# The first product of a feed-forward by seven products of quarters for five of eleven pairs of tiles, with the order of all engines written down

## The chip, the cores and the metric

One core of one Trainium2 chip runs the whole program in one launch. The metric is the device time of that launch in microseconds (us), taken as the median of several executions; a profiled execution, which has a time of its own, gives the trace. The engines are PE (matrix products), DVE (vector), ACT (scalar functions and copies), POOL (a second vector engine) and SP (which issues the DMAs).

## The reference

The program is a decoder of two layers, each a half feed-forward, a mixer and another half feed-forward, on 512 positions of 1024 features:

```python
def swiglu_ffn(x, norm_g, w_in, w_out):
    gate, up = jnp.split(rms_norm(x, norm_g) @ w_in, 2, axis=-1)
    return (jax.nn.silu(gate) * up) @ w_out
...
    for layer in range(DEPTH):
        x = x + 0.5 * swiglu_ffn(x, ffn_pre_norm[layer], ffn_pre_w_in[layer], ffn_pre_w_out[layer])
        ...            # mixer: RWKV-7 (layer 0) or dilated attention (layer 1), and attention to a memory
        x = x + y
        x = x + 0.5 * swiglu_ffn(x, ffn_post_norm[layer], ffn_post_w_in[layer], ffn_post_w_out[layer])
        if layer == N_A_LAYERS - 1:
            k_blocks, v_blocks = shared_kv_blocks(x, kv_norm, kv_w, kv_k_norm)
```

The inner width of a feed-forward is 2816, so `w_in` is 1024 x 5632 and `w_out` 2816 x 1024. All is fp32. The four feed-forwards are called 00, 01, 10 and 11 (layer, then before or after its mixer).

## The kernel before

The state x lies transposed: eight tiles of 128 features x 512 positions (part j of x is features 128 j to 128 j + 127). Weights are cut into tiles of 128 columns; a tile of the first product has eight blocks of 128x128, one for each part of x, and is loaded in two halves of four blocks (`raw`, 128x512, 256 KB).

**Split products.** PE multiplies in a rounded fp32 form, so every operand is split in a high and a low part: ACT copies it to the rounded form (`whi`, `uh`, `hh`), and DVE or POOL subtracts that from the original (`wlo`, `ul`, `hl`). Each product is then three matmuls: high by high, high of the weights by low of x, low of the weights by high of x. `weight` (line 383) loads and splits one half tile, the low part by turns on DVE and POOL; `dense` (line 401) issues the three matmuls for each block.

**A feed-forward** (`ffn`, line 444). The first product has 22 tiles of gate columns and 22 of up columns. For each m of 22 the gate tile and the up tile go through 8 blocks x 3 matmuls of 128x512 each into two banks. The square sum of x, kept by `Operand.squares`, is turned by `Operand.rstd` into the reciprocal root `r` of every position, spread on 128 partitions: one fp32 matmul of 512 columns with ones, a root on ACT, a reciprocal of 128x512 on DVE. Gating is DVE (gate times `r`, `gs`), ACT (Silu), DVE (times up, `hm`), and the hidden tile is split. The second product has eight output tiles of 22 blocks x 3 matmuls; `add_state` (line 427) scales the result, adds the old part of x, which is read again from memory (`xin`), makes the high and low parts of the next normed operand, and stores the part (`xd`).

**Beside the products.** Keys and values of the memory (256 positions) come from 96 matmuls with 256 columns, after the second product in feed-forward 00 and near the end of the first product in 01 (`memory_operand`, `memory_kv`). Feed-forward 01 also computes the position bias (`bias_rows`), and 10 reads its input again as the operand of the shared keys (`reload`: `kvh`, `kvl`). Mixer B starts from that operand and its own. At the end of each mixer, `lead` splits the first four half tiles of the next feed-forward.

**What sets the order.** Each engine runs its own list of instructions in order and waits by semaphores. The lists come from the tile framework's scheduler, which places the recorded instructions by their data and the buffers that come free; inside a mixer, `weave` with `Meter`'s costs sets the order in which strands are recorded. Weights have 6 buffers of `raw` and 4 each of `whi` and `wlo`; the feed-forward has 8 banks (`fps`).

## Time and profile before

| what | us |
|---|---|
| median of three runs (lowest, highest) | 2134.4 (2134.18, 2135.02) |
| time of the profiled execution | 2133.36 |
| its span, first to last instruction | 2131.6 |
| PE busy in the span | 2065.4 |
| feed-forward 00, from 6.2 | 379.8 |
| mixer A, from 386.0 | 419.4 |
| feed-forwards 01 and 10, from 805.4 | 740.3 |
| mixer B, from 1545.7 | 218.3 |
| feed-forward 11, from 1764.0 | 362.9 |

A row of a timeline gives the start, the length, engine, line, operation and tiles, and in brackets the idle time before it and who ended that. A row of a group gives the count (x), the busy time in all and the mean in ns, then idle time before its instructions by who ended it. The record of a matmul is longer than its share of the time, since matmuls overlap: the distance between starts is what one costs in a row of many. "L278" is the line of the helper through which every instruction of this kernel is issued (in the changed kernel the same helper is at line 309), so groups are told apart by their tiles.

### The profile page before, as it was taken

Reading aid. Unit: us, or ns where it says so; the run is one execution under the profiler, and the core shown is the slowest. Engines: PE = TensorE matmul, PEld = TensorE weight load, DVE = VectorE, ACT = ScalarE, POOL = GpSimd, SP = SyncE. Lnnn points to the kernel's source line nnn. Section 1 sums busy time; section 2 is a strip of 40 time slices with the busy share of each in tenths; the row PEclk is TensorE's granted clock in tenths of the full one; section 3 lists DMA queues with packets and bytes.
Section 4 is the critical chain, followed back from the end, with each engine's and each line's share of the span. In section 5 each row is a group of like instructions: output and inputs, shape, how many; then the busy total and the mean of one; then the engine's idle time right before and its main releaser. Section 6 shows DMA issues by size and latency. Waiting matters only on the chain.

```text
span 2131.6 us, 32197 instructions
## 1 busy us (share of the span) xinstructions
PE 2065.4 (97%) x12734; PEld 1651.9 (77%) x12734; DVE 983.3 (46%) x1354; ACT 817.6 (38%) x1408; POOL 583.1 (27%) x502
## 2 busy tenths in 40 slices
PE   8999999979989899999999999999999999999999
PEld 6888888857666577778888888888877667888887
DVE  6333343575767747333434533324376675333322
ACT  6333333423333545333433433333345654333321
POOL 2222222643332133222222222222242224222221
PEclk9999999999999999999999999999999999999999
DMA  5322344311100045253344423234441144222342
GB/s 194 97 97 96 92 136 126 117 46 34 34 27 24 24 152 188 93 183 99 109 127 126 158 95 98 95 94 135 125 136 50 38 161 156 96 97 96 94 136 82
DMA packets 130632, 221.90 MB, mean 104 GB/s; under 512 B 14232, under 2 KB 31824, under 8 KB 130480
## 3 DMA queue, kind: packets, MB, share of 16 engines
q1 hardware_dynamic: 130480, 219.83, 32.8%
q8 instruction: 100, 1.64, 0.3%
q14 instruction: 52, 0.43, 0.1%
HBM read 202.89 MB, written 21.61 MB: 105 GB/s over the span
## 4 chain that ended last, share of the span: by engine, by line
PE 62%; DVE 2%; ACT 1%; issue 1%; DMA 0%; POOL 0%; SPq 0%; POOLq 0%; ACTq 0%; DVEq 0%
PE fps L278 50%; PE mm L278 6%; PE sc L278 4%; PE py L278 1%; DMA xin<-xd 0%; DVE prob L278 0%; DVE x L278 0%; DVE tmp L278 0%; DVE ul L278 0%; ACT krv L278 0%; DVE wlo L278 0%; DVE dmx L278 0%; POOL wlo L278 0%; DVE mpr L278 0%; ACT tmp L278 0%
## 5 line engine op out<-in xcount | busy, mean ns | idle before, releaser
L278 POOL TENSOR_TENSOR wlo<-raw,whi 128x512 fp32r<-128x512 f32 (+3 forms) x404 | 496.3, 1230 | 1439.7 <-ACT whi L278 1395.2
L278 ACT ACTIVATE whi<-raw 128x512 fp32r<-128x512 f32 (+3 forms) x684 | 416.1, 610 | 955.1 <-PE fps L278 778.7
L278 PE MATMUL fps<-uh,whi 128*128 128x512 f32 x1408 | 551.9, 392 | 7.6 <-ACT whi L278 7.6
L278 PE MATMUL fps<-uh,wlo 128*128 128x512 f32 x1408 | 550.0, 391 | 4.0 <-DVE wlo L278 2.4
L278 PE MATMUL fps<-ul,whi 128*128 128x512 f32 x1408 | 549.2, 390 | 0.0
L278 DVE TENSOR_TENSOR wlo<-raw,whi 128x512 fp32r<-128x512 f32 x280 | 201.2, 719 | 347.0 <-ACT whi L278 337.3
L278 PEld LDWEIGHTS fps<-uh,whi 128*128 128x128 f32 x1408 | 264.9, 188 | 68.3 <-ACT whi L278 11.1
L278 PEld LDWEIGHTS fps<-uh,wlo 128*128 128x128 f32 x1408 | 264.9, 188 | 62.0 <-DVE wlo L278 4.1
L278 PEld LDWEIGHTS fps<-ul,whi 128*128 128x128 f32 x1408 | 265.0, 188 | 56.0 <-issue 0.7
L278 PE MATMUL fps<-hh,whi 128*128 128x512 f32 x704 | 273.9, 389 | 0.0
L278 PE MATMUL fps<-hl,whi 128*128 128x512 f32 x704 | 273.9, 389 | 0.0
L278 PE MATMUL fps<-hh,wlo 128*128 128x512 f32 x704 | 273.9, 389 | 0.0
L278 DVE TENSOR_TENSOR gs<-fps,rstd 128x512 f32<-128x512 f32 x88 | 60.5, 690 | 322.9 <-PE fps L278 322.9
L278 PEld LDWEIGHTS fps<-hh,whi 128*128 128x128 f32 x704 | 132.1, 188 | 27.5
L278 PEld LDWEIGHTS fps<-hh,wlo 128*128 128x128 f32 x704 | 132.1, 188 | 27.4
L278 PEld LDWEIGHTS fps<-hl,whi 128*128 128x128 f32 x704 | 132.1, 188 | 27.4
L278 PE MATMUL mm<-uh,whi 128*128 128x512 f32 x280 | 120.6, 431 | 1.3 <-DVE x L278 0.9
L278 DVE TENSOR_TENSOR hm<-fps,gs 128x512 f32<-128x512 f32 x88 | 60.6, 691 | 121.5 <-PE fps L278 115.8
L278 PE MATMUL mm<-ul,whi 128*128 128x512 f32 x280 | 114.7, 410 | 1.1 <-DVE ul L278 1.1
L278 PE MATMUL mm<-uh,wlo 128*128 128x512 f32 x280 | 113.3, 405 | 0.0
L278 DVE RECIPROCAL tmp<-tmp 128x128 f32<-128x128 f32 x112 | 97.8, 918 | 29.1 <-ACT tmp L278 29.0
L278 DVE TENSOR_TENSOR hl<-hm,hh 128x512 fp32r<-128x512 f32 x88 | 76.9, 877 | 50.7 <-ACT hh L278 50.7
(256 smaller groups left out, 2115.5 us busy)
## 6 DMA issues: line engine op xcount, KB each, us to landing
raw<-w SPq DMA_DIRECT2D x512, 256.0 KB, 2.7
raw<-wa_in SPq DMA_DIRECT2D x44, 256.0 KB, 3.0
xd<-x SPq DMA_DIRECT2D x40, 256.0 KB, 3.8
tmp<-xd SPq DMA_DIRECT2D x32, 256.0 KB, 3.7
xin<-xd SPq DMA_DIRECT2D x32, 256.0 KB, 4.2
raw<-w_kv SPq DMA_DIRECT2D x24, 256.0 KB, 2.8
raw<-w SPq DMA_DIRECT2D x32, 128.0 KB, 2.3
raw<-wmem SPq DMA_DIRECT2D x16, 256.0 KB, 2.6
```

Source lines behind the costliest of these rows:

```text
L278: r = f(*args, **kw)
```

## The change

**The products.** In the first product of each feed-forward, five of the eleven pairs of hidden tiles (p = 1, 3, 5, 7, 9; a pair has two gate and two up tiles) are computed by seven products of quarters in place of eight. The quarters of the weights of one m are "11" and "12" (gate, even and odd parts of x) and "21" and "22" (up); x is quartered into even and odd parts, first and second half of the positions. Sums of weight quarters (S1 = 21 + 22, S2 = S1 - 11, S3 = 11 - 21, S4 = 12 - S2) are made on POOL, from further loads (`sraw`). Each product is two jobs, one for each m of the pair, of four blocks x three matmuls of 128x256. Sums of the results are formed by ACT copies and DVE additions. The other six pairs (class `Whole`) keep 128x512 matmuls; their x of an even part holds the first half and the difference of the second half to the first, and `copy` and `finish` undo that difference.

**The operands.** An even part of x is split in two halves (`Operand.add` with `turns`), and three turned operands t2, t3, t4 are built early in the feed-forward (`turns`: x is loaded again, then per two parts an ACT scaling, three DVE instructions, two ACT copies and two DVE subtractions).

**The order.** `ffn` records under a manual schedule: every engine's list is the order in which the code is written, job by job. A job is one half tile and its twelve matmuls. Weights are loaded up to eight jobs ahead and split three jobs ahead (`ahead, loads = 3, 8`). All low parts of a feed-forward's weights are on DVE. Jobs 0 to 7 are both first tiles (even parts, then odd), jobs 8 to 11 a third tile, and the first pair begins at job 12; between the products of a pair one job of a whole tile is put.

**The root.** `column` uses four fp32 matmuls of one column, a root and a reciprocal of 128x4, and `spread` four fp32 matmuls of 128x128 that put it on 128 partitions, and a copy on ACT.

**What moves.** The memory's products and keys go between output tiles of the second product (00 and 01); the bias rows to the second product of 01 in nine parts of 256 columns, and their copies to that of 10; the loading of the shared keys' operand from feed-forward 10 to the start of mixer B. Feed-forward 10's first half tiles are split at the end of 01 (`follow`).

The diff, cut to its core:

```diff
@@ class Operand
+        if self.turns and j % 2 == 0:
+            d = net.xp.tile([P, TH], F32, tag="turn", bufs=1, name=net.nm("turn"))
+            net.split_into(h[:, :TH], l[:, :TH], x[:, :TH], gain)
+            nc.vector.tensor_tensor(d, x[:, TH:], x[:, :TH], op=ALU.subtract)
+            net.split_into(h[:, TH:], l[:, TH:], d, gain)
+        else:
+            net.split_into(h, l, x, gain)
...
-        nc.tensor.matmul(ps[:, :n], net.ones, self.acc, start=True, stop=True)
+        for b in range(n // P):
+            nc.tensor.matmul(ps[:, b:b + 1], self.acc[:, b * P:(b + 1) * P], net.ones[:, :1], start=True, stop=True,
...
+    def spread(self, c, ps):
+        for b in range(n // P):
+            nc.tensor.matmul(ps[:, b * P:(b + 1) * P], c[:, b:b + 1].broadcast_to([P, P]), net.ident, start=True,
...
@@ class Net
+    def both(self, raw, eng=None):
+        self.nc.scalar.activation(hi, raw, AF.Copy)
+        (eng or self.nc.vector).tensor_tensor(lo, raw, hi.bitcast(F32), op=ALU.subtract)
...
+            act.activation(a, a, AF.Copy, scale=self.v(gain, 2 * i))
+            yield
+            vec.scalar_tensor_tensor(b[:, 1], b[:, 1], g, a[:, 1], op0=ALU.mult, op1=ALU.subtract)
+            vec.tensor_tensor(a[:, 0], b[:, 1], a[:, 0], op=ALU.add)
+            vec.scalar_tensor_tensor(b[:, 0], b[:, 0], g, a[:, 0], op0=ALU.mult, op1=ALU.subtract)
...
+            form = {1: ("11", b11), 2: ("12", b21), 3: ("S4", b22), 5: ("S1", t1)}
...
+                def sum(q, i, n):
+                    a, b, op = {"S1": ("21", "22", ALU.add), "S2": ("S1", "11", sub), "S3": ("11", "21", sub),
+                                "S4": ("12", "S2", sub)}[n]
+                    t = self.take(hp, [P, WB, P], F32, "S", 6)
+                    gp.tensor_tensor(t, q.S[i, a], q.S[i, b], op=op)
...
+                    elif n == 6:
+                        q.s2 = tile_g()
+                        vec.tensor_tensor(q.s2, q.Y(), q.s1, op=ALU.add)
+                    elif n == 7:
+                        vec.tensor_tensor(q.s3, q.Y(), q.s1, op=ALU.add)
+                        vec.tensor_tensor(q.s3, q.Z(), q.s3, op=ALU.add)
...
+            seven = [p for p in range(1, NF // 2) if p % 2 == 1 and p < NF // 2 - 1]
+            order = (1, 5, 2, 6, 7, 4, 3)
...
+                for n in order:
+                    starts[p, n] = len(jobs)
+                    jobs += q.jobs(n)
+                    if others and (n != 1 or p == seven[0]):
+                        jobs.append(others.pop(0))
...
+            ahead, loads = 3, 8
...
+                if c + ahead < len(jobs) and c + ahead >= 8:
+                    both(jobs[c + ahead])
+                if j.then:
+                    j.then()
...
+                elif 5 < c < 16:
+                    for i in range(KD // 2):
+                        if 0 <= c - 6 - 2 * i < 4:
+                            next(steps[i], None)
@@ mixer_b
+            run(self.reload(ukv, src))
```

The lists of three engines in the first product of feed-forward 11 show where things now stand. PE, before, at the end of one tile's chain and the start of the next (`fps` is a bank, `uh` and `ul` the parts of x):

```order
L278 MATMUL fps_15951<-ul_15736,whi_16008 128x512
L278 MATMUL fps_15951<-uh_15735,wlo_16009 128x512
L278 MATMUL fps_15951<-uh_15741,whi_16008 128x512
L278 MATMUL fps_15951<-ul_15742,whi_16008 128x512
L278 MATMUL fps_15951<-uh_15741,wlo_16009 128x512
L278 MATMUL fps_16033<-uh_15617,whi_16037 128x512
```

PE, now, within the first pair, at the end of one job and the start of the next, whose weights are a sum:

```order
L309 MATMUL fps_19032<-ul_18174,whi_19002 128x256
L309 MATMUL fps_19032<-uh_18173,wlo_19003 128x256
L309 MATMUL fps_19076<-uh_18043,whi_19025 128x256
L309 MATMUL fps_19076<-ul_18044,whi_19025 128x256
L309 MATMUL fps_19076<-uh_18043,wlo_19026 128x256
```

The matmuls of a pair have half the columns and one job has twelve of them. DVE, before, just behind the reciprocal of the root (`gs` and `hm` gate, `hl` is a hidden low part):

```order
L278 RECIPROCAL rstd_15929<-rstd_15929 128x512
L278 TENSOR_TENSOR wlo_16038<-raw_16035,whi_16037 128x512
L278 TENSOR_TENSOR gs_15932<-fps_15803,rstd_15929 128x512
L278 TENSOR_TENSOR gs_15941<-fps_15805,rstd_15929 128x512
L278 TENSOR_TENSOR hm_15935<-fps_15804,gs_15932 128x512
L278 TENSOR_TENSOR hm_15944<-fps_15806,gs_15941 128x512
```

DVE, now, a stretch of the 32 instructions between the first turning step and the low part of job 15 (`h` of 256 columns is a turning step or gating, `tl` a turned low part):

```order
L309 TENSOR_TENSOR wlo_18479<-raw_18346,whi_18478 128x512
L309 TENSOR_TENSOR wlo_18509<-raw_18348,whi_18508 128x512
L309 TENSOR_TENSOR tl_18485<-h_18257,th_18484 128x512
L309 TENSOR_TENSOR tl_18487<-h_18257,th_18486 128x256
L309 SCALAR_TENSOR_TENSOR h_18256<-h_18256,vec 128x256
L309 TENSOR_TENSOR h_18256<-h_18256 128x256
L309 SCALAR_TENSOR_TENSOR h_18256<-h_18256,vec 128x256
L309 TENSOR_TENSOR wlo_18538<-raw_18363,whi_18537 128x512
L309 TENSOR_TENSOR g_18482<-fps_18457,g_18482 128x256
L309 TENSOR_TENSOR h_18249<-fps_18457,rstd_18451 128x256
L309 TENSOR_TENSOR h_18249<-g_18482,rstd_18451 128x256
L309 TENSOR_TENSOR wlo_18568<-raw_18398,whi_18567 128x512
```

Between two low parts there now stand the steps of the turned operands and the gating in halves. POOL, before, at the same place, has every second low part of the weights:

```order
L278 TENSOR_TENSOR wlo_16009<-raw_16006,whi_16008 128x512
L278 TENSOR_TENSOR wlo_16056<-raw_16053,whi_16055 128x512
L278 TENSOR_TENSOR wlo_16092<-raw_16089,whi_16091 128x512
L278 TENSOR_TENSOR wlo_16139<-raw_16136,whi_16138 128x512
L278 TENSOR_TENSOR wlo_16175<-raw_16172,whi_16174 128x512
```

POOL, now (`S` is a sum; the row of `h` is a hidden low part):

```order
L309 TENSOR_TENSOR S_18532<-sraw_18412,sraw_18414 128x512
L309 TENSOR_TENSOR S_18563<-sraw_18434,sraw_18436 128x512
L309 TENSOR_TENSOR h_18535<-h_18247,hh_18534 128x512
L309 TENSOR_TENSOR S_18617<-S_18532,sraw_18470 128x512
L309 TENSOR_TENSOR S_18643<-sraw_18470,sraw_18412 128x512
L309 TENSOR_TENSOR S_18670<-S_18563,sraw_18506 128x512
L309 TENSOR_TENSOR S_18690<-sraw_18506,sraw_18434 128x512
```

POOL's low parts have gone to DVE, and sums and hidden low parts stand in their place.

More of the change, by code (lines that the diff above doesn't have):

```diff
@@ new lines, in ffn @@
+            last_turn = starts[seven[-1], 3]
+            jobs += others
+            n1 = len(jobs)
+            there = {m: max(c for c, j in enumerate(jobs) if j.m == m) + 4 for m in range(NF)}
+            at = 0
+            for m in range(NF):
+                early = m < NF - 2 * slots
+                at = max(at + (10 if early else m % 2), there[m], 0 if early else last_turn)
+                mark(at, lambda e=gp if early or m % 2 else vec: split_hidden(e))
+            before, products, after = second(tmp, extra) if second else ((), [], ())
@@ L504, in memory_kv @@
[L504 to L519 removed]
+        have, ps = {}, {}
@@ L1217, in trunk, with rest @@
+                    return tuple(t[:, j % 2] for t in tiles[j - j % 2])
+                before, products, after = net.memory(layer, tmp, bank, place, out)
+                def rest():
+                    yield from after
+                    if more:
+                        yield from more(tmp, lambda t: bank())
+                return before, products, rest()
+            return pool, out, parts
         nxt = Operand(net, "g0m")
-        pool, kv, before, after = memory(0)
+        pool, kv, steps = memory(0)
```

515 lines of the change are left out of this document (391 added, 124 removed).

## The prediction

> **What bounds the kernel now.** I read the page's first part, then busy time by stage, then the waits of PE.
>
> ```profile
> span 2131.6 us, 32197 instructions
> PE 2065.4 (97%) x12734; PEld 1651.9 (77%) x12734; DVE 983.3 (46%) x1354; ACT 817.6 (38%) x1408; POOL 583.1 (27%) x502
> ...
> 0.00:6.20 6.20, 0.00 (x0) 0.00 (x0) 0.75 (x1) 3.25 (x5) 0.34 (x6) 1.00 0.61 182
> 6.20:386.00 379.80, 377.42 (x1693) 312.11 (x1693) 149.04 (x204) 148.40 (x246) 95.04 (x76) 1.00 0.39 121
> 386.00:805.40 419.40, 379.99 (x5061) 279.73 (x5060) 270.81 (x396) 160.26 (x303) 151.20 (x148) 0.98 0.18 58
> 805.40:1545.70 740.30, 739.70 (x3289) 608.18 (x3288) 286.76 (x375) 270.28 (x443) 180.19 (x146) 1.00 0.39 121
> 1545.70:1764.00 218.30, 207.61 (x1112) 154.61 (x1111) 153.07 (x222) 118.49 (x226) 65.12 (x57) 1.00 0.32 100
> 1764.00:2126.90 362.90, 360.49 (x1587) 297.29 (x1585) 121.45 (x156) 116.87 (x188) 91.24 (x73) 1.00 0.34 107
> ...
> PE fps L278 <- ACT whi L278: 7.6, 2, 6.2
> PE fps L278 <- DVE wlo L278: 2.4, 2, 1.6
> ```
>
> After 6.2 us of loads the five stretches are the first feed-forward, mixer A, the second and third feed-forwards, mixer B and the last feed-forward; the columns are length, then busy time of PE, PEld, DVE, ACT and POOL, granted clock, DMA share, GB/s. The feed-forwards fill 1483.0 us, and PE is busy in 1477.6 of them: only PE's own work can be cut there, and any new wait of PE is added in full. The clock is 1.00, so a shorter wait of PE buys nothing back. The two wait rows say how little PE waits for split weights today. The profiled execution took 2133.36 us for a span of 2131.6; it lies 1.0 under the median of 2134.4, and the sum below is made against it.
>
> **The products, the one gain.** For four 128-column tiles the kernel now issues 4 x 8 x 3 = 96 matmuls with 512 columns of x; a pair by seven products issues 7 x 2 x 4 x 3 = 168 with 256. So all hangs on the pitch of the two widths. Both stand in the first feed-forward (PE's timeline; the second width in the memory keys):
>
> ```profile
> 329.69 0.39 PE L278 MATMUL fps<-hh,whi 128*128 128x512 f32 x1
> ...
> 339.89 0.39 PE L278 MATMUL fps<-hh,whi 128*128 128x512 f32 x1
> ...
> 373.21 0.28 PE L278 MATMUL fps<-mh,whi 128*128 128x256 f32 x1
> ...
> 379.44 0.28 PE L278 MATMUL fps<-ml,whi 128*128 128x256 f32 x1
> ...
> L278 PEld LDWEIGHTS fps<-mh,wlo 128*128 128x128 f32 x64 | 12.3, 192 | 0.0
> ```
>
> Of 512 columns there are 46 rows from the first to the last, (339.89 - 329.69) / 45 = 0.2267 us apart; of 256 there are 53, (379.44 - 373.21) / 52 = 0.1198 us. The weight load of 192 ns does not set the narrow pitch: loads overlap. A pair costs 168 x 0.1198 = 20.13 us and not 96 x 0.2267 = 21.76, 1.64 less. Five pairs in four feed-forwards: **-32.7 us**. The other six pairs keep their 96 matmuls.
>
> [...]
>
> **The root of the mean square.** One fp32 matmul of 512 columns becomes four that make a column (128x1) and, after a reciprocal, four that spread it (128x128).
>
> ```profile
> 827.87 1.02 PE L278 MATMUL fps<-sq,cst 128*128 128x512 f32 x2
> 828.33 0.80 PE L278 MATMUL fps<-uh,whi 128*128 128x512 f32 x1
> 828.97 0.40 PE L278 MATMUL fps<-ul,whi 128*128 128x512 f32 x1
> ...
> 1054.03 0.60 PE L278 MATMUL fps<-cst,mt 128*128 128x128 f32 x4
> 1054.39 0.48 PE L278 MATMUL fps<-uh,whi 128*128 128x512 f32 x1
> ```
>
> The old one takes 828.97 - 827.87, less the one matmul between at 0.2267, so 0.87 us. The spread has the same 512 fp32 columns and is put at the same 0.87. The column is new: an fp32 matmul leaves two records (the x2 above), so eight, for which the nearest row is the four of 128x128 at (1054.39 - 1054.03) / 4 = 0.09 a record: 0.72 us. Six full ones and two of half width: 6 x 0.72 + 2 x 0.36 = **+5.0** (ends +2, if a 128x1 record costs a third of that; +12, if each of its 28 matmuls costs half an old one, 0.435). In the feed-forwards two weight jobs stand between column and spread, 5.4 us of cover (a job is one tile of weights, four blocks by three matmuls: 12 x 0.2267 = 2.72 us at 512 columns, 1.44 at 256). In mixer A the order puts only three matmuls (0.68 us) between column and spread, while ACT's root, DVE's reciprocal and three hand-overs lie between them; I add **+0.7** (0 to 2). The old reciprocal of 512 columns on DVE goes, off PE's path.
>
> **The early stretch of each feed-forward.** This is where I expect the loss. All low parts of its weights move to DVE, POOL gets the sums S1 to S4 of weight quarters, and in jobs 6 to 15 DVE also builds the turned operands and gates the first two tiles at once. Prices of the pieces (busy, mean ns of one):
>
> ```profile
> L278 DVE TENSOR_TENSOR wlo<-raw,whi 128x512 fp32r<-128x512 f32 x280 | 201.2, 719 | 347.0 <-ACT whi L278 337.3 <-PE fps L278 9.3
> L278 DVE TENSOR_TENSOR gs<-fps,rstd 128x512 f32<-128x512 f32 x88 | 60.5, 690 | 322.9 <-PE fps L278 322.9
> L278 DVE TENSOR_TENSOR mt<-fps,rstd 128x256 f32<-128x256 f32 x8 | 3.4, 422 | 7.8 <-PE fps L278 7.8
> L278 DVE SCALAR_TENSOR_TENSOR ml<-mt,vec,mh 128x256 fp32r<-128x256 f32 x16 | 7.9, 501 | 6.2 <-ACT mh L278 6.1
> L278 POOL TENSOR_TENSOR wlo<-raw,whi 128x512 fp32r<-128x512 f32 x340 | 447.6, 1317 | 1223.1 <-ACT whi L278 1182.3 <-PE mm L278 16.1 <-ACT WU L278 9.9
> L278 DVE TENSOR_TENSOR hl<-hm,hh 128x512 fp32r<-128x512 f32 x88 | 76.9, 877 | 50.7 <-ACT hh L278 50.7
> L278 ACT ACTIVATE whi<-raw 128x512 fp32r<-128x512 f32 x620 | 389.5, 630 | 886.6 <-PE fps L278 755.4 <-PE mm L278 103.8 <-issue 13.0
> ```
>
> Let T be the start of job 8. From the first turning step to the low part that job 15 (the first sum) needs, DVE has 32 instructions in order: five low parts and two turned low parts of 512 columns (7 x 0.719), six scaled subtractions of 256 (6 x 0.501), nineteen others of 256 (19 x 0.422), together 16.1 us. The first three, 1.4, can run before the spread result is there, about 1.3 after T. PE comes to job 15 at T + 4 x 2.72 + 2 x 1.44 + 2.72 = T + 16.5. On its own DVE ends at about T + 16, and with four hand-overs from ACT (the two turned low parts of each of two steps), 50.7 / 88 = 0.58 each as in the row of hl, at about T + 18: **1.5 late**. In the same stretch POOL has five instructions of the 1317-ns kind, and these two engines get in each other's way:
>
> ```profile
> 269.22 1.29 POOL L278 TENSOR_TENSOR wlo<-raw,whi 128x512 fp32r<-128x512 f32 x1 [2.79 <-ACT whi L278]
> ...
> 269.42 1.65 DVE L278 TENSOR_TENSOR x<-x,xin 128x512 f32<-128x512 f32 x1
> ...
> 1763.22 1.59 POOL L278 TENSOR_TENSOR wlo<-raw,whi 128x512 fp32r<-128x512 f32 x1
> 1764.78 3.45 POOL L278 TENSOR_TENSOR sq<-sq,sq 128x512 f32<-128x512 f32 x2
> 1770.77 1.36 POOL L278 TENSOR_TENSOR wlo<-raw,whi 128x512 fp32r<-128x512 f32 x1 [2.54 <-ACT whi L278]
> ...
> 1763.59 1.77 DVE L278 TENSOR_TENSOR wlo<-raw,whi 128x512 fp32r<-128x512 f32 x1
> ...
> 1766.98 1.87 DVE L278 TENSOR_TENSOR qn<-sc,tmp 128x512 f32<-128x512 f32 x3
> ...
> 1770.92 1.75 DVE L278 TENSOR_TENSOR wlo<-raw,whi 128x512 fp32r<-128x512 f32 x1
> ...
> 1765.41 0.50 PE L278 MATMUL fps<-uh,wlo 128*128 128x512 f32 x1 [0.85 <-DVE wlo L278]
> 1772.73 0.50 PE L278 MATMUL fps<-uh,wlo 128*128 128x512 f32 x1 [1.56 <-DVE wlo L278]
> ```
>
> DVE instructions with both inputs in SBUF (the x addition, two low parts) take 1.65 to 1.77 us where POOL runs beside them, and end about half a microsecond after POOL does; the three with an input in PSUM at 1766.98 take 0.62 each beside the same engine. The two PE rows show it reach PE: 1.56 for one encounter. Behind the late low part stand on DVE all the following ones, and PE waits for them in turn. I take the 1.5 of DVE alone and one encounter of 1.6 per feed-forward: 4 x 3.1 = **+12.4**. Ends: 0 if DVE's hand-overs are hidden and POOL falls into gaps, 4 x 7 = 28 if four and more of POOL's instructions (1.32 each) block DVE there.
>
> **The rest of the first product.** One pair with its six interleaved jobs takes PE 14 x 1.44 + 6 x 2.72 = 36.5 us. DVE has in it 20 low parts, nine gating instructions of 512 and nine of 256 columns: 20 x 0.719 + 9 x 0.690 + 9 x 0.422 = 24.4. POOL has eight sums and about two hidden low parts, 10 x 1.317 = 13.2. Even end to end that is 37.6, and the nine gating ones of the first kind, which read PSUM, can lie beside POOL. I take **0**; the ends are 0 and 1.1 a pair, 22 in all. Split weights stand three jobs ahead, at least 4.3 us, against an estimated 1.9 for a split (0.630 + 0.58 + 0.719, from the rows above). DMA carries 20 loads of 256 KB a pair, 144 GB/s; the 6.2 us ahead of the first matmul show 182, so nothing is added.
>
> **Starts and mixer B.** Before each feed-forward an even part of x costs DVE two scaled subtractions of 256 and one subtraction (2 x 0.501 + 0.422) in place of one of 512 (0.719, priced as a low part), +0.7 each and 2.7 for four; the last feed-forward's first low parts, two of which POOL made, also go to DVE (+1.4). Its two stalls of 0.85 and 1.56 then grow, by 4.1 at most, and so do the second's; the third starts from weights split in the tail before, so the 0.6 that PE isn't busy in the second and third together can fall away. I take **+2** (-2 to +8). The shared keys' operand is now loaded again at mixer B's start:
>
> ```profile
> L278 ACT ACTIVATE kvh<-xin,vec x8: 707/723/724, 1185.6 to 1206.9; 128x512 fp32r<-128x512 f32 x8
> ...
> L278 PE MATMUL mm<-kvh,whi x116: 387/389/799, 1566.2 to 1757.8; 128*128 128x512 f32 x116
> ```
>
> Eight parts took 21.3 us from first to last before, and PE first reads them 20.5 us after mixer B starts, part by part: **+1** (0 to 4). Bias rows (nine matmuls of 256 for four of 512 and one of 256) keep their columns, and the memory keys keep their 96 matmuls in another place: 0 (ends 0 and 1).
>
> **Sum.** -32.7 + 5.0 + 0.7 + 12.4 + 0 + 2 + 1 = -11.6, from 2133.4: 2121.8, so **2122 us**. With the likeliest terms moving by themselves it is 2111 to 2130.
>
> **Rivals.** (1) *Nothing is late.* The early stretch is hidden, since DVE is free ahead of it and the hand-overs overlap: 2133.4 - 11.6 - 12.4 = 2109. For it speaks that DVE is 46% busy and that its sum of 16.1 is just under what is due; against it the 1.56 row, where one encounter was enough. (2) *Slower: POOL's sums block DVE inside every pair.* The order in the pair is fixed, so DVE meets a PSUM result that is late, stands, and then finds POOL in the way; a low part comes one POOL instruction late, and PE waits for it at each of the twenty pairs. With one of 1.32 a pair it is 26 more: 2148; with two, 2174. It decides from 11.6 / 20 = 0.58 us a pair. For it: 37.6 against 36.5 above, nearly no slack if all is serial. Against it: the three-job lead, and PE's 2.4 us of waits for DVE in all feed-forwards now, though there DVE has 280 low parts beside POOL's 340. (3) *About the same.* The early stretch costs 5 to 6 a feed-forward, or pairs 0.4 to 0.5 each: 2130 to 2138. (4) *Narrow matmuls go at the pace of their weight loads*, since half as many columns hide each load: 168 x 0.192 = 32.3 us a pair, +10.5 x 20, 2332. The 52 intervals speak against it.
>
> [...]
>
> **Chances and range.** Forecast 0.42, rival (1) 0.20, (2) 0.24, (3) 0.12, (4) 0.02. A change of this kernel can be told from none at about 0.2%, 4.3 us: faster is under 2130.1, slower over 2138.7. Forecast and (1) are faster: 0.62; (3) the same: 0.12; (2) and (4) slower: 0.26. The range runs from 2103 (rival 1 with the column cheap and the starts at -2) to 2150 (rival 2 with one sum a pair), which leaves out half of (2) and a little of (1). The forecast's own range is 2111 to 2130.
>
> **What will show it.** Right: in the pairs, runs of 256-column matmuls 0.120 us apart; PE busy lower by some 28; a gap of 2 to 4 us on PE at the first quarter products of each feed-forward, released by DVE's low part, with DVE instructions of 1.3 us and more there; hardly any gap from the second pair on. Wrong, if the gaps come back in every pair (rival 2), if none is in the early stretch (rival 1), if the waits at the narrow products are put down to ACT or to raw weights from DMA, or if mixer A or B grows by more than 3 us.

## The result: 51 us slower, and the profile after

The changed kernel took 2185.1 us (median of four, 2181.5 to 2186.3) against 2134.6 on the same chip: a ratio of 1.022 (1.0202 to 1.0238; the medians alone make 1.0237). The forecast was 2122, and the range ended at 2150. The kernel before ran again beside every experiment, with medians of 2135.1 to 2136.2, and single executions took from 2128.5 to 2141.4, longer as their mean granted clock was lower (0.998 to 0.990), so a few us between two executions tell nothing by themselves. The profiled execution took 2185.29 us with a span of 2183.5, that is 51.9 more span than before.

The first part of the changed kernel's page, with the span and the busy time of the engines:

```profile
span 2183.5 us, 36883 instructions
PE 2082.0 (95%) x14278; PEld 1717.1 (79%) x14278; DVE 1424.9 (65%) x2103; ACT 914.2 (42%) x1710; POOL 563.9 (26%) x441
```

PE has 1544 more records (1440 for the pairs, 96 for the root, 8 for the bias rows), but it is busy for 16.6 us more where 28 less were forecast, and 95% of the span where it was 97%. DVE went from 983 to 1425 us.

Busy time by stage of the changed kernel (the same five stretches as in the prediction; length, then PE, PEld, DVE, ACT, POOL, granted clock, DMA share, GB/s):

```profile
6.20:392.70 386.50, 376.54 (x2073) 325.70 (x2074) 261.59 (x393) 171.65 (x322) 86.65 (x58) 1.00 0.45 144
392.70:813.20 420.50, 381.96 (x5074) 281.72 (x5073) 270.41 (x399) 159.33 (x303) 151.83 (x148) 0.97 0.18 58
813.20:1575.10 761.90, 745.97 (x4052) 638.38 (x4051) 501.11 (x740) 313.07 (x583) 169.38 (x114) 0.99 0.45 141
1575.10:1805.40 230.30, 217.44 (x1125) 159.98 (x1125) 154.75 (x232) 122.50 (x235) 65.67 (x57) 0.96 0.34 105
1805.40:2179.10 373.70, 360.13 (x1961) 311.33 (x1959) 234.37 (x338) 144.24 (x264) 90.06 (x60) 0.98 0.41 131
```

Every stage grew: the first feed-forward by 6.7, mixer A by 1.1, the second and third feed-forwards together by 21.6, mixer B by 12.0, the last feed-forward by 10.8. The feed-forwards were 1483.0 long with 5.4 in which PE was not busy; now they are 1522.1, with 39.5 of that kind. And PE's busy time in them, which was to fall by 28, rose by 5: slower matmuls count as busy (records of 0.63 for 0.39 in the early stretch below). The mean granted clock of the whole execution was 0.983, before 0.995. If all that is missing from 1 was time at half rate (0.50, as in the early stretch below), that is an estimated 74 us now against 21 before; with work for PE all the while it would make up to 26 of the 52 us.

The waits of PE for low parts of weights in the changed kernel (idle time in all, number, longest):

```profile
PE fps L309 <- DVE wlo L309: 26.0, 20, 7.3
```

They went from 2.4 to 26.0. To account for the rest I split each feed-forward on PE's timeline: its matmuls by width, each count times the pitch of the prediction (0.2267 and 0.1198) as the nominal time, and what was over that by its place.

| where | us | forecast, its ends |
|---|---|---|
| matmuls at the pitches of the prediction, root included | -28.9 | -32.7 + 5.0 |
| first quarter products of each feed-forward, with the half pitch behind them | +26.8 | +12.4 (0 to 28) |
| starts, first 110 matmuls of each | +10.5 | +2 (-2 to +8) |
| matmuls of the same size at a longer pitch | +13.0 | not in the sum |
| other stalls, those behind memory loads among them | +17.3 | 0 |
| mixer A | +1.3 | +0.7 |
| mixer B | +12.2 | +1 (0 to 4) |
| sum | +52.2 | -11.6 |

Where one of the middle four rows ends and the next begins is a choice. With other bounds, and with 1.1 put down to the root, the same trace gives +27.9, +11.7, +11.4 and +15.4 for them, so each is good to about 2 us; their sum is not in doubt.

Three questions follow: what holds the early stretch, where the longer pitch comes from, and what costs 12 in mixer B and 10 in the starts.

**The early stretch.** The timeline of the changed kernel in the last feed-forward: first POOL's sums of weight quarters, then DVE beside them with one free instruction for comparison, then PE, and last two windows, of this stretch and of the pairs behind it:

```profile
1849.66 1.47 POOL L309 TENSOR_TENSOR S<-S,sraw 128x512 f32<-128x512 f32 x1
1851.09 1.49 POOL L309 TENSOR_TENSOR S<-sraw,sraw 128x512 f32<-128x512 f32 x1
1852.53 1.47 POOL L309 TENSOR_TENSOR S<-S,sraw 128x512 f32<-128x512 f32 x1
1853.96 1.45 POOL L309 TENSOR_TENSOR S<-sraw,sraw 128x512 f32<-128x512 f32 x1
...
1849.90 1.51 DVE L309 SCALAR_TENSOR_TENSOR h<-h,vec 128x256 f32<-128x256 f32 x1
1851.45 1.40 DVE L309 TENSOR_TENSOR h<-h 128x256 f32<-128x256 f32 x1
1852.89 1.39 DVE L309 SCALAR_TENSOR_TENSOR h<-h,vec 128x256 f32<-128x256 f32 x1
1854.20 1.75 DVE L309 TENSOR_TENSOR wlo<-raw,whi 128x512 fp32r<-128x512 f32 x1
...
1860.04 0.48 DVE L309 SCALAR_TENSOR_TENSOR h<-h,vec 128x256 f32<-128x256 f32 x1
...
1856.01 0.39 PE L309 MATMUL fps<-uh,wlo 128*128 128x256 f32 x1 [2.13 <-DVE wlo L309]
...
1858.78 0.63 PE L309 MATMUL fps<-ul,whi 128*128 128x512 f32 x1
1859.20 0.63 PE L309 MATMUL fps<-uh,wlo 128*128 128x512 f32 x1
1859.63 0.63 PE L309 MATMUL fps<-uh,whi 128*128 128x512 f32 x1
...
1854.00:1868.00 14.00, 9.99 (x49) 8.07 (x50) 11.44 (x22) 7.46 (x16) 2.70 (x2) 0.88 0.24 75
1868.00:2007.00 139.00, 139.00 (x908) 127.21 (x908) 110.46 (x148) 60.67 (x112) 59.39 (x38) 1.00 0.44 145
```

POOL's four sums stand end to end, 1.43 us apart, and DVE gets one instruction through for each: the four take from 1849.90 to 1855.95, 6.05 us, where their prices in the prediction add up to 2.1 (0.501 + 0.422 + 0.501 + 0.719). The low part that ends last releases PE at 1856.01 after 2.13 of waiting. Then comes a second cost: matmuls of 512 columns start 0.43 apart (1858.78, 1859.20, 1859.63), not 0.2267, and the granted clock of that window is 0.88, and 0.50 from 1857.85 to 1861.25. The whole stretch loses 7.5, 6.8, 6.9 and 7.0 us in the four feed-forwards. In the second window, which holds the rest of the pairs, PE is busy in all of 139 us; in the other three feed-forwards it is idle for 0.2 to 1.4 us there.

### The profile page after: what moved, and what is told of

It reads as the page before. It is cut to its first block, busy times and chain, and to the rows that moved or that the text cites. A ratio compares the mean times of both kernels' runs of the same rounds, so it can differ in the third digit from the quotient of the medians.

```text
span 2183.5 us, 36883 instructions
## 1 busy us (share of the span) xinstructions
PE 2082.0 (95%) x14278; PEld 1717.1 (79%) x14278; DVE 1424.9 (65%) x2103; ACT 914.2 (42%) x1710; POOL 563.9 (26%) x441
## 5 line engine op out<-in xcount | busy, mean ns | idle before, releaser
L309 DVE TENSOR_TENSOR wlo<-raw,whi 128x512 fp32r<-128x512 f32 (+1 forms) x520 | 424.7, 834 | 305.8 <-ACT whi L309 297.3
L309 ACT ACTIVATE whi<-raw 128x512 fp32r<-128x512 f32 (+2 forms) x644 | 382.9, 605 | 492.2 <-PE fps L309 266.5
L309 PE MATMUL fps<-uh,wlo 128*128 128x512 f32 (+1 forms) x1408 | 488.4, 347 | 26.1 <-DVE wlo L309 26.0
L309 PE MATMUL fps<-uh,whi 128*128 128x512 f32 (+1 forms) x1408 | 488.5, 347 | 10.1 <-ACT uh L309 8.0
L309 PE MATMUL fps<-ul,whi 128*128 128x512 f32 (+1 forms) x1408 | 486.2, 345 | 2.6 <-DVE ul L309 2.6
L309 POOL TENSOR_TENSOR wlo<-raw,whi 128x512 fp32r<-128x512 f32 (+3 forms) x124 | 149.5, 1211 | 571.2 <-ACT whi L309 532.0
L309 PE MATMUL fps<-h,whi 128*128 128x512 f32 x704 | 276.9, 393 | 0.0
L309 PE MATMUL fps<-th,whi 128*128 128x256 f32 (+1 forms) x528 | 169.2, 320 | 4.2 <-ACT whi L309 4.2
L309 PE MATMUL fps<-th,wlo 128*128 128x256 f32 (+1 forms) x528 | 167.7, 318 | 0.0
L309 PE MATMUL fps<-tl,whi 128*128 128x256 f32 (+1 forms) x528 | 167.7, 318 | 0.0
```

The lines of the kernel that those rows point to most:

```text
L309: r = f(*args, **kw)
```

## The experiments

Where no code is shown otherwise, an edit is made on the changed kernel. Each group of experiments had runs of the kernel before on its own chip, and the ratios are against those. "Less" and "more" compare medians with the 2185.1 of the changed kernel, which was not run again beside them; differences of 5 or 6 us are near the limit of what that can tell.

### The sums taken away, the addresses put back, the pair put later, no pairs

My theory after the result: POOL's sums, by holding up DVE, make the early stretch; and the longer pitch has to do with where the moving operand lies, since small new tiles (the column of the root, the 48-byte table of the bias) had shifted all later tiles. In the built program weights and x start at 32 bytes past a multiple of 256 in both kernels. The hidden and turned tiles start at 32 as well before, but at 96 (feed-forwards 00 and 11) or 160 (01 and 10) in the changed kernel.

The small tiles to the constants' pool, with a filler behind:

```diff
-        c = net.xp.tile([P, T // P], F32, tag="rcol", ...
+        c = net.cp.tile([P, T // P], F32, tag="rcol", ...
-        rel = pool.tile([32, 12], F32, tag="rel", ...
+        rel = self.cp.tile([32, 12], F32, tag="rel", ...
+        self.cp.tile([P, 32], F32, name="pad")
```

> Edit: the two 16-byte tiles of the root's column and the 48-byte table of the position bias move from the pools in front of the feed-forward's tiles to the constants, padded to 256 bytes, so that every operand of PE again starts at 32 modulo 256 bytes, as before the change (in the changed kernel the second product's operands start at 96 or 160). Nothing else changes. Theory (the 512-column pitch rose from 0.2267 to 0.229-0.237 us because of the operands' addresses): the second products go back to 0.2267, 528 x 0.0022 to 0.0066 in each feed-forward, about 13 us in all with the whole tiles; 2185 becomes 2172. Rival (the pitch rose because DVE, DMA and PE are busier in SBUF): the pitch stays, 2185.

Measured: 2175.0 against 2135.1, ratio 1.0189 (1.0174 to 1.0205), so 10 less than the changed kernel. The pitch is seen in the third feed-forward's second product, 1519.6 to 1529.9 us, in PE's timeline. The changed kernel, first and last of 45 rows:

```profile
1519.62 0.39 PE L309 MATMUL fps<-kvl,whi 128*128 128x512 f32 x1
...
1529.89 0.39 PE L309 MATMUL fps<-hh,wlo 128*128 128x512 f32 x1
```

With the tiles put back, first and last of 46 rows:

```profile
1519.64 0.39 PE L309 MATMUL fps<-h,whi 128*128 128x512 f32 x1
...
1529.84 0.39 PE L309 MATMUL fps<-h,whi 128*128 128x512 f32 x1
```

10.27 / 44 = 0.2334 against 10.20 / 45 = 0.2267. The engines' order did not change; only addresses did. That the edit takes the longer pitch away is shown; what about the address counts is tested further down.

POOL's sums left out; a quarter is loaded into the sum's tile instead (the sums of weight quarters are not computed; the loads of the quarters that were to be summed are left out in return, so there are as many loads, and each is issued four jobs ahead of where its sum stood):

```diff
-                    gp.tensor_tensor(t, q.S[i, a], q.S[i, b], op=op)
+                    nc.sync.dma_start(t, quarter(2 * q.p + i, {"S1": "21", "S2": "22", "S3": "11", "S4": "12"}[n]))
```

> Edit: POOL makes no sums S1 to S4; each sum's tile is loaded with one of its quarters instead (left out: the weight sums, so these products are of other weights). The loads are as many as before. Theory (in the early stretch the four sums of the first pair lock DVE out, instruction by instruction): the stalls at the first quarter products, 6.2 us in each feed-forward with the half clock behind them, fall to 1 to 2; 2185 becomes about 2167. Rival (DVE alone is late there, by its own sum of 16 us): 4 us or more of each stall remain, 2180 or more. If sums also cost PE in later pairs, more than 25 us are won.

Measured: 2164.9, ratio 1.0141 (1.0126 to 1.0156), so 20 less. DVE's timeline in the last feed-forward of this kernel, the same four instructions as in the fence above:

```profile
1834.04 0.47 DVE L309 SCALAR_TENSOR_TENSOR h<-h,vec 128x256 f32<-128x256 f32 x1
1834.55 0.43 DVE L309 TENSOR_TENSOR h<-h 128x256 f32<-128x256 f32 x1
1835.01 0.49 DVE L309 SCALAR_TENSOR_TENSOR h<-h,vec 128x256 f32<-128x256 f32 x1
1835.41 0.69 DVE L309 TENSOR_TENSOR wlo<-raw,whi 128x512 fp32r<-128x512 f32 x1
```

With POOL idle they take 2.06 from first start to last end, where it was 6.05. The early stretch falls from 7.0 to 2.4 a feed-forward, 4 x 4.6 = 18 of the 20. So POOL's sums held DVE up. What is left, 2.4, are two waits of 0.7 to 1.0 for low parts, with no matmuls at half pace behind them: DVE stands there for 0.9 to 1.2 us at a time until ACT has copied the weights (`whi`), and ACT's copy is queued behind the turned copies, which wait for DVE.

The first pair three jobs later, to have POOL's sums clear of the turned operands:

```diff
-            for _ in range(4):
+            for _ in range(7):
```

> Edit: three more jobs of whole tiles (8.2 us of PE) stand ahead of the first pair, taken from those behind the last; the turning steps stay at jobs 6 to 15. Theory (the early stretch is only short of time, by 3 to 5 us, since turning steps, gating and sums fall together): most of its 25 us go away, 2185 becomes about 2162. Rival (the collision moves along with the pair, since the sums are placed by the pair's first job): the stalls stay within 2 us each, 2180 or more.

Measured: 2195.8, ratio 1.029 (1.0273 to 1.0307): 11 more, not less. PE's timeline in the first feed-forward of this kernel:

```profile
142.61 0.39 PE L309 MATMUL fps<-uh,wlo 128*128 128x256 f32 x1 [1.86 <-DVE wlo L309]
...
272.00 0.50 PE L309 MATMUL fps<-h,whi 128*128 128x512 f32 x1 [0.90 <-POOL h L309]
284.48 0.79 PE L309 MATMUL fps<-th,whi 128*128 128x512 f32 x1 [3.35 <-ACT whi L309]
```

The early stretch fell to about 5, but waits of 2.6 to 2.8 moved along with the pair, and new ones came in later pairs (142.61). At the start of the second product a hidden tile was late (272.00), but not because of POOL, which had been idle for 8.81: ACT's copy of that tile stood behind a part of the memory that waited 2.27 for its DMA. The 3.35 at 284.48 is such a memory part as well, as in the changed kernel itself (below). The theory that time alone frees DVE was wrong: the sums go with the pair, so the encounter does too.

No pairs: all 22 tiles by eight products, nothing turned, no sums; everything else as in the change:

```diff
-            seven = [p for p in range(1, NF // 2) if p % 2 == 1 and p < NF // 2 - 1]
+            seven = []
```

> Edit: no pair by seven products, all 44 tiles by eight in the new written order, so no sums, no turned operands and no 256-column matmuls in the first product. Theory (a pair saves 1.64 us on PE and the early stretch costs 25 in all): +32.7 - 25, 2185 becomes about 2193; the pitch of the second products stays high and the starts too. Rival (the pairs save what was forecast but cost it again elsewhere, in the whole tiles between): below 2175.

Measured: 2180.2, ratio 1.0214 (1.0198 to 1.0229). I had expected 13 more. The early stretch is down to 0.1 and all of the 32.7 gain is gone, and the time is 5 less than with the pairs, which the two intervals do not tell from nothing. So with sums on POOL the seven products are worth nothing: what they save on PE is given back around them. And 45 us of loss over the kernel before arise without any of them.

### The starts, mixer B, the sums on DVE, and four repairs together

The start of the last feed-forward in the changed kernel, POOL's, DVE's and PE's timelines:

```profile
1808.63 7.17 POOL L309 TENSOR_TENSOR sq<-sq,sq 128x512 f32<-128x512 f32 x5 [4.16 <-ACT sq L309]
...
1810.10 1.49 DVE L309 SCALAR_TENSOR_TENSOR ul<-qn,vec,uh 128x256 fp32r<-128x256 f32 x1
1811.51 1.75 DVE L309 TENSOR_TENSOR wlo<-raw,whi 128x512 fp32r<-128x512 f32 x1
...
1813.32 0.80 PE L309 MATMUL fps<-uh,wlo 128*128 128x512 f32 x1 [7.33 <-DVE wlo L309]
1817.01 0.80 PE L309 MATMUL fps<-uh,wlo 128*128 128x512 f32 x1 [2.04 <-DVE wlo L309]
```

The same pattern: five additions of squares on POOL, end to end, and DVE's half-width low parts take 1.49 each beside them. The squares of the feed-forwards 01 and 11 to DVE:

```diff
-            op, nxt = nxt, Operand(net, "g01", sums="gpsimd", later=True, turns=True)
+            op, nxt = nxt, Operand(net, "g01", later=True, turns=True)
```

(and the same for g11.)

> Edit: the additions of the squares of x for feed-forwards 01 and 11 go from POOL to DVE. Theory (at the start of feed-forward 11 five POOL additions, 7.17 us from 1808.63, lock DVE out of the first low parts and of the last parts of x, which take 1.5 to 1.9 us each there instead of 0.5 to 0.7): the 12.3 us that PE loses in the first 110 matmuls fall to 6 or less; 2185 becomes 2177. Rival (DVE's own list of halved parts, +0.7 us an even part, is what is late): with seven additions more on DVE it is as late as before or later, 2185 to 2190.

Measured: 2175.2, ratio 1.0193 (1.0165 to 1.022), 10 less. The same place in this kernel, DVE's and then PE's timeline:

```profile
1806.19 5.39 DVE L309 TENSOR_TENSOR sq<-sq,sq 128x512 f32<-128x512 f32 x7
...
1803.46 0.50 PE L309 MATMUL fps<-uh,wlo 128*128 128x512 f32 x1 [3.55 <-DVE wlo L309]
```

Seven additions take 5.39 on DVE (0.77 each), less than five on POOL, and the wait halves: the start of the last feed-forward loses 6.4 for 12.3, that of the second 0.1 for 3.9.

Mixer B's start in the changed kernel, ACT's and PE's timelines:

```profile
1571.32 0.72 ACT L309 ACTIVATE kvh<-xin,vec 128x512 fp32r<-128x512 f32 x1 [5.76 <-DMA xin<-xd]
...
1579.92 0.72 ACT L309 ACTIVATE kvh<-xin,vec 128x512 fp32r<-128x512 f32 x1 [2.57 <-DMA xin<-xd]
1580.55 0.70 ACT L309 ACTIVATE uh<-x,vec 128x512 fp32r<-128x512 f32 x1
...
1582.74 1.87 PE L309 MATMUL sc<-cst,sq 128*128 128x1 f32 x8 [4.25 <-DVE sq L309]
```

The reloaded parts of the shared keys' operand stand on ACT ahead of the last part of the mixer's own operand (`uh`, 1580.55), and each waits for its DMA: the square sum comes late and PE waits 4.25 for it. In the kernel before it waited 1.21 at this place:

```profile
1550.50 1.12 PE L278 MATMUL sc<-sq,cst 128*128 128x512 f32 x2 [1.21 <-DVE sq L278]
```

Here each reload is made to depend on the last `uh` (its gain is computed from that tile), so it comes behind:

```diff
+            gk, c = pool.tile([P, KD], F32, name="gk"), self.at["gkv"]
+            nc.vector.scalar_tensor_tensor(gk, u.parts[KD - 1][0].bitcast(F32)[:, :KD], 0.0, self.vec[:, c:c + KD],
+                                           op0=ALU.mult, op1=ALU.add)
+            ukv.gains = gk
             run(self.reload(ukv, src))
```

> Edit: in mixer B the splits of the reloaded operand of the shared keys are made to depend on the last part of mixer B's own operand (through their gains), so that they stand behind it on ACT and DVE; they were ahead of it in three places. Theory (mixer B grew by 12.2 us since ACT and DVE wait in order for reloaded parts, 2.5 us each, ahead of the last part of x, so the root's column is 3 us late and PE then runs at half pitch for 2): the wait of 4.25 us for the squares goes to 1.5, mixer B is 4 to 6 us shorter, 2185 becomes 2180. Rival (mixer B is longer for another reason, such as later keys): no change, or longer, since the reload ends later.

Measured: 2179.3, ratio 1.0208 (1.0183 to 1.0233), 6 less by the medians, though the interval overlaps that of the changed kernel. Surer is the trace: mixer B took 226.2 for 230.3. The wait in this kernel:

```profile
1577.49 1.05 PE L310 MATMUL sc<-cst,sq 128*128 128x1 f32 x8 [1.14 <-DVE sq L310]
```

The sums on DVE, which is to show whether POOL or the work itself is the trouble:

```diff
-                    gp.tensor_tensor(t, q.S[i, a], q.S[i, b], op=op)
+                    vec.tensor_tensor(t, q.S[i, a], q.S[i, b], op=op)
```

> Edit: DVE makes the sums S1 to S4, 40 more instructions of 0.69 us in each feed-forward; POOL keeps only hidden low parts. Theory (the lock, not the amount of work, makes the early stretch late): DVE has six sums of 0.69 more in the early stretch (4.1 us) and loses four to six lockouts of about 1 us each, so the stalls of 7 a feed-forward stay at 5 to 8, while the later pairs stay without waits (24.4 + 8 x 0.69 = 29.9 us of DVE in 36.5): 2180 to 2188. Rival (DVE is bound in the pairs once it has all sums): waits in each pair, over 2195.

Measured: 2166.4, ratio 1.0147 (1.0124 to 1.017), 19 less, nearly what leaving the sums out gave. DVE's and then PE's timeline in the last feed-forward of this kernel:

```profile
1847.31 0.48 DVE L309 SCALAR_TENSOR_TENSOR h<-h,vec 128x256 f32<-128x256 f32 x1
1848.68 0.69 DVE L309 TENSOR_TENSOR S<-sraw,sraw 128x512 f32<-128x512 f32 x1
...
1850.03 0.50 PE L309 MATMUL fps<-uh,wlo 128*128 128x512 f32 x1 [1.59 <-DVE wlo L309]
```

A sum costs 0.69 on DVE, where on POOL it took 1.47 and held DVE as long. With 40 sums a feed-forward added to its work, 28 us, DVE is earlier than in the changed kernel: the early stretch loses 3.6, with the 1.59 above as its longest wait, and the later pairs have no waits.

Four repairs together: the addresses, the squares, the reload, and the memory's loads issued two parts earlier. The last had not been tried alone; the changed kernel has this in the second product of feed-forward 01 (ACT, then PE):

```profile
1084.07 0.51 ACT L309 ACTIVATE uh<-mt,vec 128x256 fp32r<-128x256 f32 x1 [1.42 <-DMA mt<-memT]
1084.79 0.61 ACT L309 ACTIVATE whi<-raw 128x512 fp32r<-128x512 f32 x1
1085.46 0.50 PE L309 MATMUL fps<-th,whi 128*128 128x512 f32 x1 [2.90 <-ACT whi L309]
```

ACT stands at a memory part whose load was just issued, the copy of the weights is queued behind it, and PE waits 2.90 for that copy.

```diff
+            fetch(0)
+            fetch(1)
...
-                nc.sync.dma_start(x, self.ap["memT"][:, j])
-                u.add(x)
+                fetch(j + 2)
+                u.add(xs[j])
```

> Edit: together the addresses of the first experiment, squares on DVE, the reload behind x, and the loads of the memory's parts issued two parts earlier (ACT waits in order for them ahead of weight copies, 1.4 to 3.2 us at a time). Theory (these costs are separate and add): -10 -8 -5, and -4 to -6 for the memory's loads, 2185 becomes about 2157; the early stretch stays at 7 a feed-forward. Rival (they hide one another): above 2165.

Measured: 2154.0, ratio 1.0094 (1.0065 to 1.0123), 31 less; the first three alone gave 10, 10 and 6, so some 5 remain for the loads, a difference of four measured numbers and no surer than these together.

### Repairs with the sums on DVE, and what the pairs are then worth

The four repairs and the sums on DVE:

> Edit: the four repairs of the eighth experiment, and the sums S1 to S4 on DVE. Theory (the lock in the early stretch is independent of the four): 2154 less the 3.4 us a feed-forward and some of the waits at the hidden tiles that the seventh gained, about 2139. Rival (with squares and sums DVE becomes the bound): 2150 or more.

Measured: 2137.1, ratio 1.0005 (0.9993 to 1.0017). The change is level with the kernel before. From the first matmul's start to the last one's end the four feed-forwards are 377.4, 379.3, 357.3 and 364.2 long (before 380.0, 379.7, 360.8 and 363.1), and mixer B between them is 226.2 (218.1).

The first four low parts of a feed-forward behind a mixer by turns on DVE and POOL, as before, on top of that:

```diff
-        return [self.both(self.raw(w)) for w in self.begins(which)]
+        return [self.both(self.raw(w), (self.nc.vector, self.nc.gpsimd)[i % 2]) for i, w in enumerate(self.begins(which))]
```

> Edit: as the ninth, and of the first four half tiles of a feed-forward two have their low parts on POOL again, as before the change. Theory (the 5 us left at the start of feed-forward 11 are DVE's list of halved parts with four low parts in it): 2 to 3 us less there, about 2136. Rival (a low part on POOL costs 1.3 us and locks DVE): no change.

Measured: 2137.4, ratio 1.0006 (0.9992 to 1.002): no difference can be told.

That one with the first pair two jobs later (6 for 4 in the loop of the third experiment):

> Edit: as the tenth, with two more whole jobs (5.4 us) ahead of the first pair. Theory (without the lock DVE is only short of time there, by the 3.6 us a feed-forward of the seventh): the early stretch loses under 1 us a feed-forward, about 2126, unless the shorter end of the first product shows in waits at the hidden tiles, as it did in the third (then 2135). Rival (the stalls move with the pair, as in the third): 2140 and more.

Measured: 2128.7 (2126.1 to 2132.2), ratio 0.9965 (0.9951 to 0.9979): 7 us faster than the kernel before, the best of all runs. Its page and its waits of PE:

```profile
span 2124.3 us, 36684 instructions
PE 2052.9 (97%) x14278; PEld 1706.9 (80%) x14278; DVE 1410.1 (66%) x2272; ACT 921.2 (43%) x1710; POOL 310.4 (15%) x273
...
PE fps L310 <- DVE wlo L310: 5.7, 5, 4.8
```

A delay of two jobs saves 9 here, where one of three cost 11 us with the sums on POOL and the memory's loads late: the early stretch loses 1.0 to 1.4 a feed-forward, by where it is taken to end. Of the waits for low parts one of 4.8 remains, at the start of the last feed-forward. PE's busy time is 12.5 under that of the kernel before; POOL's is half of it.

The repairs of the last but one (the lead on both engines included), with no pairs:

> Edit: the four repairs and the start on both engines, with no pair by seven products (all 44 tiles by eight, no sums, no turned operands). Theory (a pair is worth its 1.64 us on PE once nothing is late): 2180 of the fourth experiment less the repairs, about 2153, so 14 to 18 above the ninth and tenth. Rival (the written order itself costs nothing once repaired): near 2140, its nominal length, 8.2 x 4 above that of the pairs.

Measured: 2154.7, ratio 1.0089 (1.0061 to 1.0117). So the pairs are worth 17 us in the kernel with the early pair and 26 in that with the later one. By the prediction's price of 32.7 the first is what four early stretches of 3.6 leave (18.3), and the second lies 1 to 3 under what four of 1.0 to 1.4 leave (28.7 to 27.1). And 20 us of loss remain beside the pairs: mixer B 7.7, the last feed-forward 5.2, the second 3.5, the first 2.9, mixer A 1.3, the third 0.3. Some 4 of mixer B's 7.7 need not be the change's (see the account of mixer B further down).

### What about the address counts

The tiles put back to equal addresses gave the old pitch. Open was whether a start at 32 matters by itself, and whether the kernel before would also slow down. Three runs: the kernel before with a filler of 64 or of 256 bytes ahead of the tiles in question, and the changed kernel with the small tiles in the constants' pool but no filler, which puts weights and moving operands all at 160.

```diff
+        net.xp.tile([P, 16], F32, tag="gap", bufs=1)     # 64 bytes; [P, 64] is 256
```

> Edit to the kernel before the change: one unused tile of 64 bytes ahead of the feed-forward's tiles, so that the hidden tiles and the shared keys' operand, which PE reads as moving operands, start at 96 modulo 256 bytes and the weights and x at 32 as before; nothing else. Theory (PE's pitch depends on where its two operands start relative to each other): the second products rise from 0.2267 to about 0.229, 4 x 528 x 0.0023 = 5 us; about 2140 where the kernel before has 2135. Rival (the first experiment gained by something else that moved with the tiles): no change.

> The same with 256 bytes: all operands at 32 modulo 256 again, at other addresses. Theory (only the offset within 256 bytes counts): 0.2267 and no change. Rival (any move of the tiles changes the pitch): as in the kernel with 64 bytes.

> Edit to the changed kernel: the small tiles go to the constants without padding, so that weights, x and hidden tiles all start at 160 modulo 256 bytes. Theory (the offset of the moving operand relative to the weights counts, not its own): as the first experiment, second products at 0.2267, about 2175. Rival (an operand at 160 is slow in itself): the pitch of 0.233 that feed-forward 10 showed with its operands at 160, everywhere, 2185 or more.

Measured: 2140.2 with 64 bytes, ratio 1.0025 (1.0015 to 1.0034); 2135.6 with 256, 0.9998 (0.9986 to 1.001); 2175.8 with all at 160, 1.0187 (1.0169 to 1.0205), as with all at 32. PE's timeline at the same place, the kernel before with 64 bytes, first and last of 46 rows:

```profile
1519.63 0.39 PE L279 MATMUL fps<-hh,whi 128*128 128x512 f32 x1
...
1529.93 0.39 PE L279 MATMUL fps<-hh,whi 128*128 128x512 f32 x1
```

And with 256 bytes, first and last of 45:

```profile
1519.82 0.39 PE L279 MATMUL fps<-hh,whi 128*128 128x512 f32 x1
...
1529.79 0.39 PE L279 MATMUL fps<-hh,wlo 128*128 128x512 f32 x1
```

10.30 / 45 = 0.2289 and 9.97 / 44 = 0.2266. In the changed kernel the second product of the last feed-forward, whose operands are 64 bytes off, has the 0.2289 too, and with all at 160 the third's is back at 0.2267. So in the kernel before, with nothing of the change in it, 64 bytes of shift cost 5 us and 256 cost nothing. Of the starts tried, what counts is the distance of the moving operand's start from that of the weights, modulo 256 bytes: 0.2267 at none, 0.2289 at 64, 0.2334 at 128. Why that is so no run tells.

## Why the prediction was wrong

The direction was wrong, by three terms that were too small and two that were not in the sum.

**The products: right.** The nominal count fell by 28.9 with the root in it, against 27.7. The narrow pitch in the pairs is 0.120, so weight loads of 0.192 us do not set it (rival 4 falls; its 2332 was also added up wrongly, since 32.3 for 20.1 is 12.1 a pair, which makes 2364). The last pair of runs gives the pairs' worth directly, 17 and 26 us, short of 32.7 by about what the early stretch takes.

**The early stretch: right in its cause, half in its size.** Gap, releaser and place were as written; the cost was 26.8 and not 12.4, at the far end of my 0 to 28. The step that failed is "one encounter of 1.6 per feed-forward". I had taken a low part's delay as one event. The rows show a queue: POOL's sums stand end to end, and DVE gets one instruction through for each of them, four in a row in the fence above (3.9 us lost there alone). Without the sums 2.4 a feed-forward are left where the prediction had 1.5 for DVE alone; with them 4.6 more, where it had 1.6. That is what I had as the upper end, four and more of POOL's instructions, and I should have seen that eight sums with their loads at hand would have no gaps between them. Beside them, the 0.43 to 0.49 of the kernel without the sums became 1.39 to 1.51 at the same width. The second part of the cost is the half pitch behind the gap, which the sum did not have at all: the prediction read the clock of 1.00 only as saying that shorter waits buy nothing back, and did not ask what longer ones cost.

**Starts: +2 became +10.5, over its end of 8.** The step assumed that two stalls grow by 4.1 at most (4.3 by its own prices). I counted only the added work on DVE and not the five additions of squares on POOL beside it, the same encounter as in the early stretch. Moving the squares to DVE took away 10 us.

**The rest of the first product: right for the changed kernel.** PE is busy in nearly all of the 138 to 141 us of the later pairs. Rival 2, with its 2174, came nearest in time, but not in place: hardly anything was lost in the pairs behind the first of each feed-forward. Rival 1 falls by the 2.13 row; what it held, that DVE alone is in time, comes nearly true only with the sums on DVE and the first pair two jobs later (1.0 to 1.4). Rival 3 asked for 5 to 6 in each early stretch and nothing elsewhere, and had neither.

**Mixer B: +1 became +12.2, beyond its end of 4.** The step looked at when PE first reads the reloaded operand, and not at what is queued behind it on ACT: the mixer's own last part, and with it the square sum. Putting the reload behind took the wait for it from 4.25 to 1.14 and gave 4 us back in the mixer. Of the other 8 most stayed in the later versions (7.7 in the repaired one without pairs, 5.0 in the fastest of all), and not all of that is the change's. Between 130 and 160 us into the mixer PE goes at half rate for a while (granted clock 0.50 from 1717.9 to 1728.1 in the changed kernel): the granted clock of 24 us there is 0.79 in the changed kernel and in the repaired one without pairs, and 1.00 in the kernel before. But the kernel before with 64 bytes of filler also has 0.79 there, behind the same waits of PE (1.63 and 0.72, for 1.67 and 0.73), and its mixer B took 222.9 for 218.1. So about 4 of the 12.2 can come to the kernel before as well; where the last 4 go was not found out.

**Costed at nothing: 17.3.** The memory products moved between output tiles, with their loads issued at the place of use. I had put the memory keys' cost at 0 to 1, by PE's matmuls alone; the parts that wait for these loads stand on ACT's queue ahead of weight copies. Issuing the loads earlier took back some 5. The rest of this row was not taken apart.

**Not in the sum: the pitch, 13.0.** No row of the kernel before could show that its 0.2267 hangs on the tiles' addresses. That the pitch is part of the loss is shown by 10 us less when the addresses are put back, and by 5 more in the kernel before with 64 bytes. The second products alone make 9 of the 10: 528 matmuls each, 0.0022 longer in two and 0.0066 in two. The other 3 or so of the 13.0 lie in the first products and stay when the addresses are put back; their cause is open.

Of the +52, then, by runs that change one thing: sums on POOL 19 to 20, addresses 10, squares 10, reload 6, and with the loads, by difference, 5. These five add up to 50 or 51; all in one kernel they gave 48. What is left with them undone nearly cancels: 32.7 gained by the pairs, 14.4 lost in four early stretches of 3.6, and 20 lost beside the pairs make +1.7, and +1.6 was measured. Only the later first pair brings the gain out, and about a fifth of it.

## What to carry to other kernels

Before work is put on POOL beside a busy DVE, count POOL's instructions that can stand end to end, not single encounters: here DVE then got one instruction through for each of POOL's, 1.43 us apart, and the same work on DVE itself can be the cheaper place, as here with 0.69 against 1.47. For a step that moves, ask what it stands ahead of on each engine that it passes, loads included, rather than when its result is first read. And when a matmul's pitch changes with no change in its shape, look at where its operands lie (0.2267 against 0.2334 here).

## What the runs showed of the hardware that was not expected

- The pitch of matmuls with 512 columns in the rounded fp32 form, in second products and of the starts tried, went with the distance of the moving operand's start from that of the weights, modulo 256 bytes: 0.2267 us at none (kernel before, both at 32; changed kernel, both at 32 or both at 160), 0.2266 with 256 bytes of filler in the kernel before, 0.2289 at 64, 0.2334 at 128.
- Longer waits of PE were followed by matmuls at half pace (0.43 for 0.2267). In the feed-forwards of all traces, past the first 30 us, none of 67 waits between 0.9 and 1.9 us was followed by any such row of matmuls, and 59 of 65 waits of 2.0 us and more were: mostly 6 to 12 of them, begun up to 4 us after the gap, while the granted clock stood at 0.50, in the changed kernel for 3.41 us at a time and once for 10.24. By that count such a stall cost an estimated 1.2 to 2.4 us more than its length (6 or 12 x 0.20, which is 0.43 less 0.2267).
- Beside POOL's four sums, which stood end to end in the changed kernel, four DVE instructions with both inputs in SBUF went through one for one: 1.39 to 1.51 us for 256 columns, 1.75 for 512. Without the sums the same four took 0.43 to 0.49 and 0.69.
- An fp32 matmul of one column left two records, which started 0.112 us apart in a row of eight (changed kernel, 29.06 to 29.73), where those of 128 columns started 0.109 apart in the kernel before (1054.03 to 1054.36): no less, and not a third, as the low end of the forecast took.
